# W_out's first blocks prepared early, the MLP entry reordered, the right factors in two pools: a float32 transformer block on one NeuronCore

## The chip, the cores and the metric

The kernel runs as one program on one core of a Trainium2 chip. Its time is the device time of one execution in microseconds, the median over several runs. A profile is taken of one execution. The engines named below are TensorE (PE, matmuls), VectorE (DVE), ScalarE (ACT), GpSimd (POOL) and SyncE (SP, which here only starts DMAs). Each engine works through its own queue in order.

## The reference, cut to what matters

One block of a transformer, 1024 tokens of width 1024, everything in float32. Two attentions (a compressed, selected and windowed one, and a sliding one with sinks) give `o_a` and `o_b`; what follows them is the part that this case is about:

```
y = sigmoid(gate_a) * (o_a @ w_up_nsa) + sigmoid(gate_b) * (o_b @ w_up_swa)
h = h + rms_norm(y @ w_out, norm_mix_post)          # w_out 1024 x 1024
u = rms_norm(h, norm_mlp_pre)
f = square(relu(u @ w_mlp_in)) @ w_mlp_out          # 1024 x 4096, 4096 x 1024
h = h + rms_norm(f, norm_mlp_post)
```

## The kernel before, in words

**Precision.** Every float32 operand is split in two: a part h, which ACT rounds to the matmul's format, and a rest l = value - h, which DVE (sometimes POOL) subtracts. A product then is three matmuls, h·h, h·l and l·h (`split`, L84; `mm3`, L123). So each weight and each activation needs an ACT and a DVE instruction before PE can use it.

**Stages around the change.** (1) The gates' loop (L752): for each of eight 128-wide column blocks `dc`, the up-projections of both attentions, times the gates, split into `yh`, `yl`, one pair for the first 512 tokens (pool y0) and one for the last 512 (pool y1). (2) `out_proj` (L813), called four times with two token blocks of 128 each: it goes through W_out in eight row blocks of 128x1024. `load_w` (L96) brings a block into one of two raw places (`wraw`), ACT rounds it to `wh`, and the rest `wl` is cut between DVE and POOL in the first two calls and made by DVE alone after that. 12 matmuls use a block. (3) The norms of each token block `b`: `norm_a` adds the residual, `norm_b` scales by the second norm (L864), `norm_t` transposes on PE into the right factors of the MLP. (4) The first MLP product, `u @ w_mlp_in`, by seven products per pair of 128-column blocks instead of eight (Strassen-Winograd); 16 pairs `p`, each product 12 matmuls (`prod`, L956). Products 1 and 2 of the first four pairs (`head`, L965) need only the first 512 tokens and are issued early, between the transposes. Products 5, 3, 6, 4, 7 (`mlp1`, L1004) need right factors `bh[i]`, `bl[i]` that DVE builds from the transposes of the last tokens (`factor`, L888), and sums and differences of W_in's columns, which POOL builds (L1014, L1041). The pairs 0 and 1 run in step with the four `factor` calls; the others follow one by one. (5) The second MLP product, from L1093, works through seven products of eight 256-deep steps `kc`. Each step splits a piece of W_out of the MLP (`vh`, `vl`) and a stored piece of the first product (`fh`, `fl`), all in pool st2 with NG = 4 places of each kind.

**What sets the order.** The Tile framework orders each engine's queue with a timeline simulation, along the program's order as far as data allow. `tc.issue_after(i)` keeps instructions of i's engine behind i. Pools are stacks on the left and the right side of SBUF; a new pool overlays a closed one, and a tile waits for the old tiles that lie in its place. u1 (L929) held bh5, bl5, bh3, bl3, bh6, bl6, bh4, bl4 (8 KB each per partition) and then the two places of 8 KB that carry b12, b22 and later bh7, bl7: 80 KB from the right end. st2, 64 KB from the same end, so lies on bh3 to bl4 and on bh7, bl7.

Of the kernel before, what the change touches and what calls it, by code (L numbers as in the profile page):

```python
# [52 lines left out]
def tile_hybrid_block(ctx: ExitStack, tc: tile.TileContext, x, norm_mix_pre, norm_mix_post, norm_mlp_pre,  # L53
# [688 lines left out]
    with ExitStack() as s:  # L742
# [3 lines left out]
        yl = [p.tile([P, NB, 512], F32R, name="yl", tag="yl") for p in yp]  # L746
        s_ps = s.enter_context(ExitStack())
# [58 lines left out]
        we = s_we.enter_context(pool("we"))  # L806
        wor = w_out.rearrange("(k p) c -> p k c", p=P)
# [3 lines left out]
        started = []  # L811

        def out_proj(c, ts_, nhs, xs_=(), at=0):  # L813
            pss = {(t, nh): ps_any() for t in ts_ for nh in nhs}
            n = 1024 // (512 * len(nhs))
            for k2 in range(NB // n):
                wh, wl = load_w([(None, wor[:, n * k2:n * k2 + n, 512 * nhs[0]:512 * nhs[-1] + 512])],
                                [n, 512 * len(nhs)], *((wp2, 2) if not started else (we, WEB)), cut=CUT[c], rpool=wp2, l_eng="dve" if c else None)
# [4 lines left out]
                for j in range(n):  # L823
                    k = n * k2 + j
                    for t in ts_:
                        ts = slice(t * P, (t + 1) * P)
                        for i, nh in enumerate(nhs):
                            ns = slice(i * 512, (i + 1) * 512)
                            mm3(pss[t, nh], yh[c][:, k, ts], yl[c][:, k, ts], wh[:, j, ns], wl[:, j, ns],
                                k == 0, k == NB - 1)  # L830
            started.append(1)
            for t in ts_:
# [4 lines left out]
                for nh in nhs:  # L837
                    ns = slice(nh * 512, (nh + 1) * 512)
                    junk = we.tile([P, 512], F32, name="junk", tag="junk", bufs=1)
# [3 lines left out]
        ss2s = {}  # L843

# [16 lines left out]
        def norm_b(b):  # L861

            r2 = rstd_of(ep, ss2s[b])
            nc.vector.scalar_tensor_tensor(o1[b], hbs[b], r2, gpre, op0=ALU.mult, op1=ALU.mult)  # L864

        def norm_t(b):
# [16 lines left out]
            nc.vector.tensor_tensor(t1, pts[0], braw[b % 4, 0], op=ALU.subtract)  # L883
# [44 lines left out]
        s_u2r = s.enter_context(ExitStack())  # L928
        u1 = s_u2r.enter_context(pool("u1", side="right"))  # L929
        bh, bl = {}, {}  # L930
        for i in (5, 3, 6, 4):
            bh[i] = u1.tile([P, 4, 512], F32R, name=f"bh{i}")
            bl[i] = u1.tile([P, 4, 512], F32R, name=f"bl{i}")
# [13 lines left out]
        norm_a(7)  # L947
        norm_t(4)
# [16 lines left out]
        def head(p, fp_, whl):  # L965
# [10 lines left out]
            nc.vector.scalar_tensor_tensor(c11, c11, 0.0, c11, op0=ALU.max, op1=ALU.mult)  # L976
            nc.sync.dma_start(f_d[0][p], c11)
# [13 lines left out]
        for b in range(4):  # L991
            factor(3, b)
# [10 lines left out]

        def mlp1(p):  # L1004
            raw = []
            for e in range(2):
                r = wp2.tile([P, NB, P], F32, name="wraw", tag="wraw", bufs=2) if e == 0 else \
                    w1a.tile([P, NB, P], F32, name="wraw2", tag="wraw2", bufs=2)
                c0 = (2 * p + e) * P
                nc.sync.dma_start(r, w_mlp_in[:, c0:c0 + P].rearrange("(k p) c -> p k c", p=P))  # L1010
                raw.append(r)
            a11, a12, a21, a22 = raw[0][:, 0:4], raw[0][:, 4:8], raw[1][:, 0:4], raw[1][:, 4:8]
            sm = w1a.tile([P, 4, P], F32, name="ws", tag="ws", bufs=3)
            nc.gpsimd.tensor_tensor(sm, a21, a22, op=ALU.add)  # L1014
            early = p in pre
            if early:
                xb, c11, _ = pre[p]
                s1 = f5.tile([P, 512], F32, name="p5", tag="p5", bufs=2)
                nc.scalar.activation(s1, xb, AF.Copy)
# [20 lines left out]
            for o, i0, i1 in ((sm, sm, a11), (a12, a12, sm), (a21, a11, a21)):  # L1040
                nc.gpsimd.tensor_tensor(o, i0, i1, op=ALU.subtract)  # L1041
# [53 lines left out]
        st2 = s.enter_context(pool("st2", side="right"))  # L1095
        pq = s.enter_context(pool("ps3", space=PSUM))
# [50 lines left out]
        def product(i, bank, first, last):  # L1147

            n = NG if last and i == 7 else 1
            for k0 in [*range(NK - n), NK - n]:  # L1150
                ks = range(k0, k0 + (n if k0 == NK - n else 1))
                hl = {}
                for kc in ks:
                    src = operand(i, kc)
                    vh = st2.tile([P, 2, 512], F32R, name="vh", tag="vh", bufs=NG)
                    vl = st2.tile([P, 2, 512], F32R, name="vl", tag="vl", bufs=NG)
# [117 lines left out]
```

## Time and profile before

| | |
|---|---|
| median of 3 runs | 1553.06 us (1552.43 to 1554.15) |
| profiled execution | 1550.25 us, span 1548.5 us |
| PE busy | 1475.5 us, 95% of the span |
| DVE, ACT, POOL busy | 68%, 51%, 23% |
| mean granted clock of PE | 0.985 |

PE busy means that a matmul was under way; at the lower clock a matmul takes longer and still counts as busy. Idle time of PE, or busy time at the lower clock, is what a change can win. Of the 40 slices (38.7 us each) into which the page cuts the span, PE has 9 tenths or more in most; in the stages that the change touches it has 8 tenths in four (from 735, 813, 968 and 1200 us) and 6 in one (from 890 us).

### The profile page before, as it was taken

How to read it: one execution, taken by the hardware profiler on the slowest of the kernel's cores; microseconds unless marked ns; L12 is line 12 of the kernel's file. 1: busy time of each engine (PE TensorE's matmuls, PEld its weight loads, DVE VectorE, ACT ScalarE, POOL GpSimd, SP SyncE). 2: the span in 40 equal slices, each digit the busy share in tenths (PEclk: the TensorE clock that was granted, in tenths of full speed). 3: DMA queues.
4: the chain of work that ended last, by engine and by line, in shares of the span. 5: the costliest groups of instructions: out<-in, count | busy, mean ns of one | idle time of the engine just before them, and what ended most of it. 6: DMA issues, size and time to landing. Idle time of an engine off the chain costs nothing.

```text
span 1548.5 us, 19945 instructions
## 1 busy us (share of the span) xinstructions
PE 1475.5 (95%) x6920; PEld 1208.1 (78%) x6920; DVE 1053.7 (68%) x2086; ACT 788.3 (51%) x1525; POOL 362.6 (23%) x290
## 2 busy tenths in 40 slices
PE   6998999999999999999898969899999899999997
PEld 5897888788887788888766757688888688888886
DVE  5555774598855988646547798787667555594775
ACT  5344675598854988654346663233322334334533
POOL 3000342100001000041052035676556300000302
PEclk9999999999999999999999979999999999999999
DMA  7733125111132111174356633444444697353551
GB/s 218 252 98 87 35 50 158 46 35 41 36 99 61 40 35 42 32 257 148 108 192 233 221 116 107 155 148 166 157 137 144 220 359 270 99 194 102 164 176 55
DMA packets 162037, 204.79 MB, mean 132 GB/s; under 512 B 15120, under 2 KB 105264, under 8 KB 161936
## 3 DMA queue, kind: packets, MB, share of 16 engines
q1 hardware_dynamic: 154224, 180.68, 36.8%
q0 software_dynamic: 6992, 20.48, 3.8%
q10 hardware_dynamic: 720, 2.36, 0.4%
q8 instruction: 54, 0.88, 0.2%
q14 instruction: 47, 0.39, 0.1%
HBM read 153.02 MB, written 58.32 MB: 136 GB/s over the span
## 4 chain that ended last, share of the span: by engine, by line
PE 69%; issue 8%; DVE 6%; POOL 3%; DMA 2%; ACT 2%; DVEq 0%; POOLq 0%; ACTq 0%
PE xs L1167 10%; PE ys L1167 8%; PE mm L124 5%; PE mm L126 5%; PE mm L125 5%; PE ps L959 5%; PE ps L961 5%; PE ps L960 5%; PE pt L522 5%; PE o L535 2%; PE o L534 2%; PE s L489 2%; DMA wraw<-in_w_out_dram 2%; PE s L490 2%; PE ps L124 2%
## 5 line engine op out<-in xcount | busy, mean ns | idle before, releaser
L124 PE MATMUL mm<-uh,wh 128*128 128x512 f32 x464 | 200.2, 431 | 5.3 <-DVE qb L448 3.2
L125 PE MATMUL mm<-ul,wh 128*128 128x512 f32 x464 | 183.9, 396 | 0.0
L126 PE MATMUL mm<-uh,wl 128*128 128x512 f32 x464 | 183.7, 396 | 0.0
L91 DVE TENSOR_TENSOR tl<-pt,th 128x512 fp32r<-128x512 f32 x162 | 110.6, 687 | 42.1 <-ACT th L87 41.2
L91 POOL TENSOR_TENSOR wl<-wraw,wh 128x1024 fp32r<-128x1024 f32 x16 | 38.4, 2403 | 417.1 <-ACT wh L87 385.2
L502 ACT ACTIVATE e<-e,nm 128x256 f32<-128x256 f32 (+7 forms) x192 | 124.3, 649 | 20.0 <-DVE nm L496 19.5
L87 ACT ACTIVATE fh<-fraw 128x1024 fp32r<-128x1024 f32 x56 | 59.4, 1063 | 146.1 <-PE xs L1167 78.5
L87 ACT ACTIVATE wh<-wraw 128x1024 fp32r<-128x1024 f32 x69 | 73.1, 1059 | 113.9 <-PE mm L125 36.7
L87 ACT ACTIVATE th<-pt 128x512 fp32r<-128x512 f32 (+1 forms) x178 | 104.4, 593 | 50.6 <-PE pt L522 43.1
L91 DVE TENSOR_TENSOR fl<-fraw,fh 128x1024 fp32r<-128x1024 f32 x56 | 69.3, 1243 | 78.3 <-ACT fh L87 78.3
L1167 PE MATMUL xs<-vl,fh 128*128 128x512 f32 x256 | 100.7, 393 | 4.2 <-DVE vl L91 4.2
L126 PEld LDWEIGHTS mm<-uh,wl 128*128 128x128 f32 x464 | 87.4, 188 | 20.7
L124 PEld LDWEIGHTS mm<-uh,wh 128*128 128x128 f32 x464 | 88.0, 190 | 18.4 <-issue 3.3
L522 PE MATMUL pt<-ident,e 128*128 128x128 f32 x648 | 101.1, 273 | 0.3 <-DVE tl L91 0.2
L91 DVE TENSOR_TENSOR wl<-wraw,wh 128x1024 fp32r<-128x1024 f32 x53 | 69.7, 1315 | 46.0 <-ACT wh L87 45.8
L1167 PE MATMUL xs<-vh,fl 128*128 128x512 f32 x256 | 100.4, 392 | 0.0
L1167 PE MATMUL xs<-vh,fh 128*128 128x512 f32 x256 | 100.1, 392 | 0.0
L125 PEld LDWEIGHTS mm<-ul,wh 128*128 128x128 f32 x464 | 88.3, 190 | 11.9
L522 PEld LDWEIGHTS pt<-ident,e 128*128 128x128 f32 x648 | 80.7, 140 | 18.4 <-issue 0.9
L1190 POOL TENSOR_TENSOR cc<-cc,gB 128x512 f32<-128x512 f32 x14 | 24.3, 1762 | 268.9 <-ACT sq L1189 267.2
L87 ACT ACTIVATE ws_h<-wraw 128x512 fp32r<-128x512 f32 x48 | 30.1, 629 | 107.1 <-PE ps L960 104.8
L959 PE MATMUL ps<-bh,ws_h 128*128 128x512 f32 x192 | 76.3, 397 | 3.9 <-ACT ws_h L87 1.7
(287 smaller groups left out, 4046.4 us busy)
## 6 DMA issues: line engine op xcount, KB each, us to landing
fraw<-f_d SPq DMA_DIRECT2D x48, 512.0 KB, 3.5
wraw<-in_w_mlp_in_dram SPq DMA_DIRECT2D x36, 512.0 KB, 4.4
wraw<-in_w_out_dram SPq DMA_DIRECT2D x32, 512.0 KB, 3.6
f_d<-q SPq DMA_DIRECT2D x64, 256.0 KB, 3.7
b<-in_w_mlp_out_dram SPq DMA_DIRECT2D x32, 512.0 KB, 10.8
wraw<-in_w_in_dram SPq DMA_DIRECT2D x27, 512.0 KB, 4.6
f_d<-c SPq DMA_DIRECT2D x48, 256.0 KB, 4.3
gate_d<-gst SPq DMA_DIRECT2D x32, 256.0 KB, 2.0
```

What stands on the lines that cost most here:

```text
L87: nc.scalar.activation(h, src, AF.Copy)
L91: eng.tensor_tensor(l, src, h.bitcast(F32), op=ALU.subtract)
L124: nc.tensor.matmul(ps, ah, bh, start=first, stop=False)
L125: nc.tensor.matmul(ps, ah, bl, start=False, stop=False)
L126: nc.tensor.matmul(ps, al, bh, start=False, stop=last)
L489: nc.tensor.matmul(ps[:, :w], qs[r][:, qcol], kh, start=True, stop=False)
L502: nc.scalar.activation(e[:, :n], e[:, :n], AF.Exp, scale=-1.0, bias=nm[:, r:r + 1], accum_out=sm[:, r:r + 1])
L522: tr = nc.tensor.transpose(pt[:rows, r, :], es[r][:, off:off + rows], ident)
L959: nc.tensor.matmul(ps, ah[:, k, :], bh[i][:, k, :], start=n[0], stop=False, skip_group_check=True)
L960: nc.tensor.matmul(ps, ah[:, k, :], bl[i][:, k, :], start=False, stop=False, skip_group_check=True)
L961: nc.tensor.matmul(ps, al[:, k, :], bh[i][:, k, :], start=False, stop=n[1], skip_group_check=True)
L1167: nc.tensor.matmul(bank[t], l_[:, j, ts], r_[:, j, :], start=a_, stop=z_, skip_group_check=True)
```

## The change

Five edits. (a) The first two W_out blocks are loaded during the gates' loop (at dc = 5), and the first is split there, into a pool `wo` of its own; the first `out_proj` call splits the second block itself and loads the other six. (b) The right factors lie in two pools, u1a with bh5, bh3, bh6 and u1 with bh4 and b12/b22/bh7, and the second product's splits in two, st2 with three places of each kind and st3 with one. (c) `norm_b(6)` and `norm_b(7)` stand ahead of `norm_t(4)`; the factors' instructions are kept behind the last `norm_b` or the last transposed difference, and behind the copy L1019. (d) Relu and square of the first four heads go from one DVE to two ACT instructions, their stores from SP's to POOL's queue, and the sums and differences of pairs 0 and 1 from POOL to DVE. (e) The W_in columns of pairs 0 to 3 are loaded ahead of the pairs, those of 2 and 3 into the places of `wh`, `wl` that the heads leave.

```diff
+        wo = s_wo.enter_context(pool("wo", side="right"))
+        def wo_load(k):
+            r = wo.tile([P, 1, 1024], F32, name="wraw", tag="wraw", bufs=2)
+            nc.sync.dma_start(r, wor[:, k:k + 1, :])
+            wo_raw.append(r)
...
+                if dc == 5:
+                    wo_load(0)
+                    wo_load(1)
+                    wo_hl += [wo.tile([P, 1, 1024], F32R, name=n, tag=n) for n in ("wh", "wl")]
+                    split(*wo_hl, wo_raw[0])
...
             for k2 in range(NB // n):
-                wh, wl = load_w(...)
+                if started or k2 > 1:
+                    wh, wl = load_w(...)
+                elif k2:
+                    wh, wl = (wp2.tile([P, 1, 1024], F32R, name=n_, tag="w" + n_[1], bufs=2) for n_ in ("wh", "wl"))
+                    split(wh, wl, wo_raw[1])
+                else:
+                    wh, wl = wo_hl
...
+        u1a = s_u2r.enter_context(pool("u1a", side="right"))
         u1 = s_u2r.enter_context(pool("u1", side="right"))
         for i in (5, 3, 6, 4):
-            bh[i] = u1.tile([P, 4, 512], F32R, name=f"bh{i}")
+            bh[i] = (u1 if i == 4 else u1a).tile([P, 4, 512], F32R, name=f"bh{i}")
...
         norm_a(6)
         norm_a(7)
+        norm_b(6)
+        norm_b(7)
         norm_t(4)
...
-            nc.vector.scalar_tensor_tensor(c11, c11, 0.0, c11, op0=ALU.max, op1=ALU.mult)
-            nc.sync.dma_start(f_d[0][p], c11)
+            if p < NPRE:
+                nc.scalar.activation(c11, c11, AF.Relu)
+                nc.scalar.activation(c11, c11, AF.Square)
+            else:
+                nc.vector.scalar_tensor_tensor(c11, c11, 0.0, c11, op0=ALU.max, op1=ALU.mult)
+            (nc.gpsimd if p < NPRE else nc.sync).dma_start(f_d[0][p], c11)
...
             if p == 0:
                 norm_t(5)
-                norm_b(6)
-                norm_b(7)
...
-        for b in range(4):
-            factor(3, b)
+        with tc.issue_after(last_norm[0].ins):
+            for b in range(4):
+                factor(3, b)
...
+        def load_raw(p):
+            raw = {}
+            for e in (1, 0):
+                pool_, tag = ((w1a, "wraw2") if e else (wp2, "wraw")) if p > 3 else \
+                    ((wp2, "wraw"), (w1a, "wraw2"), (wp2, "w" + "hl"[e]), (wp2, "w" + "hl"[e]))[p]
+                raw[e] = pool_.tile([P, NB, P], F32, name="wraw", tag=tag, bufs=2)
+                c0 = (2 * p + e) * P
+                nc.sync.dma_start(raw[e], w_mlp_in[:, c0:c0 + P].rearrange("(k p) c -> p k c", p=P))
+            return raw
+        raws = {p: load_raw(p) for p in range(NPRE)}
...
-            nc.gpsimd.tensor_tensor(sm, a21, a22, op=ALU.add)
+            diff = nc.vector if p < 2 else nc.gpsimd
+            with tc.issue_after(last_t[0].ins):
+                diff.tensor_tensor(sm, a21, a22, op=ALU.add)
...
-                nc.gpsimd.tensor_tensor(o, i0, i1, op=ALU.subtract)
+                diff.tensor_tensor(o, i0, i1, op=ALU.subtract)
...
-            for b in range(4 if i else 0):
-                factor(i, b)
+            with tc.issue_after(last_t[0].ins), tc.issue_after(last_s1[0].ins):
+                for b in range(4 if i else 0):
+                    factor(i, b)
...
+        st3 = s.enter_context(pool("st3", side="right"))
+        def st_tile(name, kc):
+            p, n = (st3, 1) if kc % NG == NG - 1 else (st2, NG - 1)
+            return p.tile([P, 2, 512], F32R, name=name, tag=name, bufs=n)
...
-            h = st2.tile([P, 2, 512], F32R, name="fh", tag="fh", bufs=NG)
-            l = st2.tile([P, 2, 512], F32R, name="fl", tag="fl", bufs=NG)
+            h, l = st_tile("fh", kc), st_tile("fl", kc)
```

`last_norm`, `last_t` and `last_s1` hold the latest DVE instruction of `norm_b` (L864), of `norm_t` (L883) and the latest ACT copy L1019. The pool `we` is opened after the first `out_proj` call, when `wo` is closed.

## Rows read from the trace of the kernel before

**Rows 1.** The page's first part: busy time, share, instructions of each engine.

```profile
PE 1475.5 (95%) x6920; PEld 1208.1 (78%) x6920; DVE 1053.7 (68%) x2086; ACT 788.3 (51%) x1525; POOL 362.6 (23%) x290
```

**Rows 2.** Stretches: length, busy PE, PEld, DVE, ACT, POOL (instructions), granted clock, DMA share, GB/s.

```profile
768.90:800.20 31.30, 25.70 (x97) 19.92 (x96) 8.84 (x11) 9.83 (x10) 13.11 (x8) 0.89 0.59 204
800.20:883.80 83.60, 76.29 (x329) 57.04 (x328) 61.84 (x111) 51.61 (x91) 16.79 (x14) 1.00 0.66 226
883.80:907.80 24.00, 23.89 (x112) 19.63 (x112) 23.59 (x47) 18.08 (x36) 1.06 (x2) 1.00 0.56 167
907.80:933.80 26.00, 12.41 (x40) 8.92 (x37) 25.39 (x30) 14.61 (x27) 12.69 (x8) 0.67 0.21 61
933.80:960.00 26.20, 26.20 (x112) 20.66 (x113) 18.50 (x23) 8.05 (x14) 12.58 (x9) 1.00 0.35 102
960.00:1010.00 50.00, 44.13 (x178) 33.42 (x177) 36.95 (x36) 13.03 (x22) 34.66 (x22) 0.97 0.48 154
1224.00:1237.05 13.05, 8.08 (x25) 6.14 (x25) 10.48 (x12) 5.56 (x7) 2.17 (x3) 0.74 0.71 247
```

**Rows 3.** Waits of PE from 660 to 1010: total us, times, longest.

```profile
PE ps L124 <- ACT wh L108: 7.2, 6, 4.5
PE pt L874 <- DVE o L864: 5.9, 2, 4.7
PE ps L959 <- ACT p L1019: 4.3, 1, 4.3
PE ps L961 <- DVE s_l L91: 3.7, 1, 3.7
```

**Rows 4.** Timeline, PE, first W_out call: start, us, line, operation, [idle before, releaser].

```profile
773.44 2.07 PE L124 MATMUL ps<-wh,yh 128*128 128x512 f32 x4 [4.49 <-ACT wh L108]
...
784.70 1.10 PE L124 MATMUL ps<-wh,yh 128*128 128x512 f32 x4
...
787.50 1.10 PE L124 MATMUL ps<-wh,yh 128*128 128x512 f32 x4
```

**Rows 5.** Timeline of SP's queue, ACT and POOL in the same call.

```profile
768.31 50.89 SPq L100 DMA_DIRECT2D wraw<-in_w_out_dram  x15
...
772.33 1.06 ACT L108 ACTIVATE wh<-wraw 128x1024 fp32r<-128x1024 f32 x1 [1.26 <-DMA wraw<-in_w_out_dram]
...
786.52 1.66 POOL L116 TENSOR_TENSOR wl<-wraw,wh 128x384 fp32r<-128x384 f32 x1 [1.58 <-ACT wh L108]
```

**Rows 6.** DMA issues of the page: count, KB each, median us to landing.

```profile
wraw<-in_w_out_dram SPq DMA_DIRECT2D x32, 512.0 KB, 3.6
```

**Rows 7.** Timeline, DVE, at the MLP's entry.

```profile
911.34 1.28 DVE L864 SCALAR_TENSOR_TENSOR o<-hb,rs_o,gpre 128x1024 f32<-128x1024 f32 x1
...
914.49 0.68 DVE L896 TENSOR_TENSOR braw<-b_l,braw 128x512 f32<-128x512 f32 x1
...
920.88 1.75 DVE L895 TENSOR_TENSOR b_l<-b_l,b_h 128x512 f32<-128x512 f32 x1
```

**Rows 8.** Groups by line, DVE, 883.8 to 934.8: count, busy us, mean ns, idle before.

```profile
L91 DVE TENSOR_TENSOR bl<-braw,bh 128x512 fp32r<-128x512 f32 x8 | 7.5, 953 | 0.0
...
L976 DVE SCALAR_TENSOR_TENSOR c<-c 128x512 f32<-128x512 f32 x4 | 2.7, 680 | 0.0
```

**Rows 9.** Groups by line, POOL, the same stretch.

```profile
L1041 POOL TENSOR_TENSOR ws<-ws,wraw 128x512 f32<-128x512 f32 x2 | 3.3, 1666 | 2.5 <-DVE s_l L91 2.5
```

**Rows 10.** Line L1014 (POOL): what its idle time waited for, us, times.

```profile
  DMA wraw<-in_w_mlp_in_dram: 55.4, 14
```

**Rows 11.** Waits of SP's queue, 880 to 1010: total us, times, longest.

```profile
SPq L1010 <- DVE ws_l L91: 51.9, 10, 21.7
```

**Rows 12.** Timeline at the second product's start: ACT, DVE, PE.

```profile
1221.14 1.06 ACT L87 ACTIVATE fh<-fraw 128x1024 fp32r<-128x1024 f32 x1 [2.15 <-PE ps L961]
...
1229.85 1.22 DVE L91 TENSOR_TENSOR fl<-fraw,fh 128x1024 fp32r<-128x1024 f32 x1
...
1232.26 0.79 PE L1167 MATMUL xs<-vl,fh 128*128 128x512 f32 x1 [4.23 <-DVE vl L91]
```

More of the change, by code (lines that the diff above doesn't have):

```diff
@@ L746, in tile_hybrid_block @@
         yl = [p.tile([P, NB, 512], F32R, name="yl", tag="yl") for p in yp]
+        s_wo = s.enter_context(ExitStack())
+        wo = s_wo.enter_context(pool("wo", side="right"))
+        wor = w_out.rearrange("(k p) c -> p k c", p=P)
+        wo_raw, wo_hl = [], []
+        def wo_load(k):
+            r = wo.tile([P, 1, 1024], F32, name="wraw", tag="wraw", bufs=2)
+            nc.sync.dma_start(r, wor[:, k:k + 1, :])
+            wo_raw.append(r)
         s_ps = s.enter_context(ExitStack())
@@ L805, in tile_hybrid_block @@
         s_we = s_e.enter_context(ExitStack())
-        we = s_we.enter_context(pool("we"))
-        wor = w_out.rearrange("(k p) c -> p k c", p=P)
         ssp = [ep.tile([P, 2], F32, name="ssp", tag="ssp", bufs=8) for _ in range(NB)]
         hbs = {}
-        started = []
+        started, we = [], []
         def out_proj(c, ts_, nhs, xs_=(), at=0):
@@ L816, in out_proj @@
             for k2 in range(NB // n):
-                wh, wl = load_w([(None, wor[:, n * k2:n * k2 + n, 512 * nhs[0]:512 * nhs[-1] + 512])],
-                                [n, 512 * len(nhs)], *((wp2, 2) if not started else (we, WEB)), cut=CUT[c], rpool=wp2, l_eng="dve" if c else None)
+                if started or k2 > 1:
+                    wh, wl = load_w([(None, wor[:, n * k2:n * k2 + n, 512 * nhs[0]:512 * nhs[-1] + 512])],
+                                    [n, 512 * len(nhs)], *((we[0], WEB) if started else (wp2, 2)), cut=CUT[c],
+                                    rpool=wp2, l_eng="dve" if c else None)
+                elif k2:
[3 more added lines that the diff above has]
+                    wh, wl = wo_hl
                 if k2 == at:
@@ L830, in out_proj @@
                                 k == 0, k == NB - 1)
+            if not started:
+                s_wo.close()
+                we.append(s_we.enter_context(pool("we")))
             started.append(1)
@@ L838, in out_proj @@
                     ns = slice(nh * 512, (nh + 1) * 512)
-                    junk = we.tile([P, 512], F32, name="junk", tag="junk", bufs=1)
+                    junk = we[0].tile([P, 512], F32, name="junk", tag="junk", bufs=1)
                     nc.scalar.activation(junk, pss[t, nh], AF.Square, accum_out=ssp[b][:, nh:nh + 1])
@@ L843, in tile_hybrid_block @@
         ss2s = {}
+        last_norm, last_t, last_s1 = [None], [None], [None]
         def load_x(b, eng=None):
@@ L863, in norm_b @@
             r2 = rstd_of(ep, ss2s[b])
-            nc.vector.scalar_tensor_tensor(o1[b], hbs[b], r2, gpre, op0=ALU.mult, op1=ALU.mult)
+            last_norm[0] = nc.vector.scalar_tensor_tensor(o1[b], hbs[b], r2, gpre, op0=ALU.mult, op1=ALU.mult)
         def norm_t(b):
@@ L882, in norm_t @@
             t1 = eh.tile([P, 4, P], F32, name="t1", tag="hb", bufs=2)
-            nc.vector.tensor_tensor(t1, pts[0], braw[b % 4, 0], op=ALU.subtract)
+            last_t[0] = nc.vector.tensor_tensor(t1, pts[0], braw[b % 4, 0], op=ALU.subtract)
             nc.scalar.activation(b12[:, :, bs], pts[0], AF.Copy)
@@ L931, in tile_hybrid_block @@
         for i in (5, 3, 6, 4):
-            bh[i] = u1.tile([P, 4, 512], F32R, name=f"bh{i}")
-            bl[i] = u1.tile([P, 4, 512], F32R, name=f"bl{i}")
+            bh[i] = (u1 if i == 4 else u1a).tile([P, 4, 512], F32R, name=f"bh{i}")
+            bl[i] = (u1 if i == 4 else u1a).tile([P, 4, 512], F32R, name=f"bl{i}")
         def u7(name, dt):
@@ L1002, in ab @@
                     p_.tile([P, 4, P], F32R, name=tag + "l", tag=tag + "l", bufs=bufs))
-        def mlp1(p):
[L1005 to L1011, printed above, removed]
+        def load_raw(p):
[8 more added lines that the diff above has]
+        raws = {p: load_raw(p) for p in range(NPRE)}
+        def mlp1(p):
+            raw = raws[p] if p in raws else load_raw(p)
             a11, a12, a21, a22 = raw[0][:, 0:4], raw[0][:, 4:8], raw[1][:, 0:4], raw[1][:, 4:8]
             sm = w1a.tile([P, 4, P], F32, name="ws", tag="ws", bufs=3)
-            nc.gpsimd.tensor_tensor(sm, a21, a22, op=ALU.add)
+            diff = nc.vector if p < 2 else nc.gpsimd
+            with tc.issue_after(last_t[0].ins):
+                diff.tensor_tensor(sm, a21, a22, op=ALU.add)
             early = p in pre
@@ L1018, in mlp1 @@
                 s1 = f5.tile([P, 512], F32, name="p5", tag="p5", bufs=2)
-                nc.scalar.activation(s1, xb, AF.Copy)
+                last_s1[0] = nc.scalar.activation(s1, xb, AF.Copy)
             else:
@@ L1154, in product @@
                     src = operand(i, kc)
-                    vh = st2.tile([P, 2, 512], F32R, name="vh", tag="vh", bufs=NG)
-                    vl = st2.tile([P, 2, 512], F32R, name="vl", tag="vl", bufs=NG)
+                    vh, vl = st_tile("vh", kc), st_tile("vl", kc)
                     hl[kc] = f_op(i, kc) + (vh, vl)
```

## Prediction

> **What bounds the kernel now.** The page's first part comes first: PE is busy for 1475.5 of 1548.5 us [rows 1], so whatever this change wins it wins from the 73 us in which PE is idle, and from matmuls that ran at the lower clock. Next come the stretches [rows 2], to find where those losses lie. The price of a matmul there comes from the timeline: two W_out blocks of 12 matmuls each begin at 784.70 and 787.50 [rows 4], so a matmul of 512 columns costs 2.80 / 12 = 0.233 us when nothing is late. What each stretch takes beyond its matmuls at that price is its loss:
>
> - 768.9 to 800.2, the first W_out call: 96 matmuls are 22.4 us of 31.3; lost 8.9.
> - 800.2 to 883.8, the other three calls: 329, of them 40 transposes, which I price at half a matmul (an estimate); 72.1 of 83.6; lost 11.5.
> - 907.8 to 960.0, from the last head to the end of the first pairs: 152, of them 16 transposes; 33.6 of 52.2; lost 18.6.
> - 960 to 1010: 178 are 41.5 of 50; lost 8.5.
> - 1224 to 1237, the turn to the second product: 25 are 5.8 of 13.05; lost 7.2.
>
> Third, the waits of PE [rows 3] say what ended last in them: ACT's rounding of the first W_out block (4.5 us at once), `norm_b`'s output (4.7 us), the copy L1019 (4.3 us) and DVE's rest `s_l` (3.7 us). Each gap is followed by matmuls at the lower of the two clocks, 1.2 GHz: the granted clock is 0.89, 0.67 and 0.74 in the stretches with gaps and 1.00 in those without [rows 2]. A gap removed gives back this part too, and the loss figures hold it. Four of the five losses are aimed at by the change: 8.9 + 18.6 + 8.5 + 7.2 = 43.2 us.
>
> **(a) First W_out blocks.** Now SP can start the first W_out load only at 768.31, since its place lies on the attention outputs that the gates' last matmuls read; ACT begins at 772.33 [rows 5] and PE at 773.44 after 4.49 us of idleness [rows 4]. With block 0 split at dc = 5, PE goes on at 769. Block 1 needs only its split: 1.06 us of ACT [rows 5] and 1.22 us of DVE [rows 12], within the 2.8 us of block 0; at worst ACT takes the gates' last `yh` first and PE waits 0.6 us (an estimate). The two loads (3.6 us each [rows 6]) and block 0's split are hidden by the gates' loop, where PE never waits for ACT or DVE; without that cover they would cost about 2.4 us. Can the loads of blocks 2 and on follow? The chain of one raw place is load 3.6, ACT 1.06, POOL 1.66 [rows 5, 6], 6.3 us for every second block or 3.2 per block against PE's 2.8. So this ring falls behind by 0.4 us a block, but it starts two blocks ahead: it has 14 blocks in the first two calls instead of 16, which is 6.3 us, plus the raw places, which come free about 2 us earlier (they now lie on operands that the gates read earlier in their last group). By the ring the gain is 8.3 us, by PE's loss it is at most 8.9. Bounds 5 and 9; I take 7.5.
>
> **(b) Two pools.** At the second product's start PE waits 4.23 us for `vl`, behind `fl` at 1229.85 [rows 12]. The place of `fl` was bh7's, which the last product reads to its end; `fh` lay on bh4 and started at 1221.14 when product 4 let go [rows 12]. With 48 KB for st2 on the 48 KB of u1a, the first three steps' splits wait for products 5, 3 and 6 alone, and only step 3 (16.8 us of matmuls later) waits for product 7. So `fl` and `vl` of step 0 can run in product 7's 2.8 us: 2 x 1.22 us [rows 12], just enough. The price: DVE's queue may still hold the last pair's evictions ahead of them, worth 1 to 3 us. At the entry bh5 and b12/b22 now lie on y1, which the last W_out call reads to its end, instead of on free ground; the instructions that write them came after that end anyway, so I put 0 to 1 us on it. Bounds 1 and 7; I take 6 of 7.2.
>
> **(c, d) The entry.** From 883.8 to 933.8 DVE is busy for 23.59 + 25.39 = 49.0 of 50 us [rows 2], and does its work in the wrong order: `norm_b(7)` came at 911.34 [rows 7], after many factors that PE needed only from 934 on, while the last transposes, on which every factor product hangs, waited for it. With both `norm_b` ahead and the factors held behind, norm, eviction and `norm_t` work up to the last transposed difference fits into the 24 us of heads. Then DVE's total: less L976, 2.7 us [rows 8] (ACT takes eight instructions for it, 0.6 us each by estimate from 1.06 for twice the width [rows 5], and has 17 idle us in the two stretches [rows 2]); plus eight differences at 0.68, 5.4 us; less what POOL cost it. That last term is read off the same operations: 0.68 us alone, 1.75 beside POOL's [rows 7], and a mean of 0.953 for the eight `bl` [rows 8]. POOL's eight differences (12.69 us in 907.8 to 933.8 [rows 2], 1.67 each [rows 9]) could so stretch eight DVE operations by 1.07, up to 8.6 us. So 49.0 - 2.7 + 5.4 - 8 = 43.7 us if POOL stays quiet. After the heads 43.7 - 24 = 20 us are left, plus 12 further splits and evictions, 8 us, against the 10 x 2.8 = 28 us of the products of pairs 0 and 1: balanced, with a hand-over of 2 to 4 us at the first product and some lateness at product 6, whose factor needs three DVE operations per token block. I leave 8.6 of the 18.6 lost: gain 10, bounds -5 (the order makes DVE wait) and 16.
>
> The stores of the four heads go past SP's queue, where they stood between W_in loads, to POOL's, which has 1.06 us of work in the 24 us of heads [rows 2]; nothing of POOL's is late for them.
>
> The Trainium skill ("SBUF — State Buffer", section "Who interferes with whom") says that a DVE instruction with two SBUF inputs and a GpSimd instruction that reads SBUF lock each other out, whichever starts first. Here DVE's 1.75 us beside POOL's 1.67 agree [rows 7, 9]. The rule speaks against (e) as much as for (d): the differences of pairs 2 and 3 stay on POOL and now find their data early. By it the first rival below holds; by the rows of the quiet DVE alone the sum above does.
>
> **(e) W_in columns.** POOL sat 55.4 us in 14 waits for these loads [rows 10], and SP held them back for 51.9 us until DVE had finished with a place [rows 11]. With the places of `wh` and `wl`, free when heads 2 and 3 are done, pairs 2 and 3 load by the end of the heads, at 908, and no longer wait for pairs 0 and 1; pairs 4 and 5 find the places of those two. A load then is early by more than one pair (19.6 us). What is late next is DVE beside POOL, busy 36.95 and 34.66 of 50 us [rows 2]. On SP's queue the eight loads stand in a row and a late place holds those behind it, which are later pairs. Of 8.5 lost I take 4.5 as gained; bounds 0 and 8.
>
> **Sum.** 7.5 + 6 + 10 + 4.5 = 28.0. The profiled execution took 1550.25, so 1522.25; the runs' median lies 2.8 above it, so 1525.
>
> **Rivals.**
> 1. Contention comes back at the entry. Pairs 2 and 3 have four differences that wait for no split; beside DVE's factors they add 4 x 1.07 = 4.3 us, all eight 8.6, where DVE has no slack. For: DVE at 49.0 of 50 [rows 2]. Against: POOL could work while DVE reads PSUM. Then entry 3 and W_in columns 2.5: 7.5 + 6 + 3 + 2.5 = 19, 1534.
> 2. DVE keeps ahead throughout and nearly every aimed loss goes: 8.5 + 7 + 15 + 7.5 = 38, 1515. For: DVE falls to 18.50 of 26.2 just after [rows 2]. Against: the narrow handing over between ACT and DVE for each split.
> 3. It doesn't do what it says: the planner still puts the last transposes behind the heads, and `fl` behind the last evictions. Entry 2, pools 1.5: 7.5 + 2 + 1.5 + 4.5 = 15.5, 1537.5. For: it is what the queues held before [rows 7, 12]. Against: the edits fix that order by hand.
> 4. Slower: the factors, held behind the last transposed difference, run in series. If that difference comes at 914 as now (L896 on its factor at 914.49 [rows 7]), 52 DVE operations at 0.68 and 8.6 of contention end at 958, and with hand-overs (6) and the last products (5.6) pairs 0 and 1 end at 970, against about 956 now (136 matmuls are 11.3 products by 960). That is 14 us, and 5 more if the gaps hold the clock at 1.2 GHz; (e) is then worth nothing. 19 - 7.5 - 6 = 5.5 slower, 1558.5. It decides from the point where the last transposes wait for the fourth head and DVE has nothing else to do. Against: DVE then would idle ahead of 914, and the norms ahead exclude just that.
>
> **How the numbers follow.** Forecast (1519 to 1530) 0.58, rival 1 0.20, rival 2 0.08, rival 3 0.09, rival 4 0.05. The range takes in the forecast, rival 2, rival 1 and part of rival 3: 1514 to 1540. A measurement of this kernel tells 0.2% (3.1 us) from no change. Forecast and rivals 1 to 3 lie below that; of rival 4 I put one part in five on a draw. With 0.01 of rival 3 also put there, faster is 0.94, same 0.02, slower 0.04.
>
> **What would show it.** In the profile after: PE has no gap ahead of its first W_out matmul and no lower clock there; the two L864 of blocks 6 and 7 stand on DVE before the second head ends; PE's waits for L864, L1019 and `s_l` are below 5 us together; POOL's L1014 waits less than 30 us for loads; the wait at the second product's start is below 1.5 us. The prediction is wrong if the losses of 907.8 to 960 merely move to the next stretch, if DVE shows new 1.75 us operations among the factors, or if the three later W_out calls lose more than 11.5 us and give (a) back.

## The result and the profile after

The changed kernel takes 1536.62 us (median of 4 runs, 1535.4 to 1538.22) against 1553.61 before; ratio 0.9892, interval 0.9875 to 0.9909. Timed once more on another chip it took 1538.79 against 1552.87, ratio 0.991 (0.9894 to 0.9926). So it is faster by 14 to 17 us; forecast were 28 (1525), and 1534 was what the first rival gave. The profile after is of an execution of 1536.7 us with a span of 1534.9.

First come the page's busy times, then the stretches, cut at about the same places of the program as in [rows 2] (columns as there):

```profile
PE 1472.4 (96%) x6920; PEld 1205.2 (79%) x6920; DVE 1044.1 (68%) x2090; ACT 793.1 (52%) x1533; POOL 347.5 (23%) x284
```

```profile
768.90:795.00 26.10, 24.52 (x104) 18.66 (x102) 8.51 (x11) 9.58 (x11) 10.31 (x7) 1.00 0.62 220
795.00:878.70 83.70, 76.34 (x328) 56.56 (x327) 61.65 (x112) 50.81 (x90) 16.34 (x14) 1.00 0.65 224
878.70:903.50 24.80, 24.80 (x121) 20.30 (x119) 21.48 (x43) 19.62 (x42) 2.70 (x5) 1.00 0.75 221
903.50:960.00 56.50, 40.11 (x147) 30.20 (x146) 51.02 (x64) 26.55 (x46) 24.42 (x16) 0.85 0.32 95
960.00:1010.00 50.00, 50.00 (x217) 40.33 (x216) 41.42 (x45) 17.26 (x27) 35.19 (x24) 1.00 0.43 148
```

The first W_out call and 960 to 1010 are mended: the clock is 1.00 and PE is busy nearly throughout. What is left of the entry's loss stands in 903.5 to 960: PE is busy for 40 of 56.5 us, DVE for 51. PE's waits from 660 to 1010, which answer to [rows 3] (L1060 was L1019, L899 was L874, L990 was L961), say the same:

```profile
PE ps L988 <- ACT p L1060: 9.3, 1, 9.3
PE ps L988 <- ACT ws_h L87: 3.5, 2, 2.4
PE ps L124 <- ACT wh L108: 3.0, 5, 1.2
PE ps L990 <- DVE ws_l L91: 2.4, 2, 2.1
...
PE pt L899 <- DVE rs_t L147: 1.2, 1, 1.2
```

The wait for the norm (4.7 at once before) is gone and the copy's has grown from 4.3 to 9.3. DVE's timeline at the end of the heads shows why (start, length, line, operation, idle time before it):

```profile
902.75 0.69 DVE L908 TENSOR_TENSOR t<-pt,braw 128x512 f32<-128x512 f32 x1 [1.94 <-PE pt L899]
903.36 0.68 DVE L1055 TENSOR_TENSOR ws<-wraw 128x512 f32<-128x512 f32 x1
907.98 0.69 DVE L1055 TENSOR_TENSOR ws<-wraw 128x512 f32<-128x512 f32 x1 [3.94 <-DMA wraw<-in_w_mlp_in_dram]
908.59 1.89 DVE L920 TENSOR_TENSOR b_l<-b_l,b_h 128x512 f32<-128x512 f32 x3
910.40 0.68 DVE L1004 TENSOR_TENSOR c<-ps,s 128x512 f32<-128x512 f32 x1
911.00 0.68 DVE L1082 TENSOR_TENSOR wraw<-wraw 128x512 f32<-128x512 f32 x1
911.60 0.68 DVE L91 TENSOR_TENSOR bl<-t,bh 128x512 fp32r<-128x512 f32 x1
```

Pair 1's sum stands at the head of DVE's queue and waits 3.94 us for its columns. Three factor differences follow (one row, L920), and only behind them come the sum of head 3 (L1004) and block 7's `bl`. ScalarE's queue waits for the sum of head 3: its ReLU and square stand there ahead of the copy that PE needs. PE starts at 912.97. At the second product the wait for `vl` (4.23 [rows 12]) has become one for the PSUM bank that the last pair's copy frees:

```profile
PE xs L1214 <- ACT c L1099: 2.3, 1, 2.3
```

To see where time is won, I take the start of the k-th matmul in each profile; all have 6920. The numbers are "before minus this one", in us (positive: earlier than before). The 4200th (counted from 0) stands just ahead of the heads and the 4700th where PE no longer waits. The second product starts at the 5576th; the 5780th and the 5850th lie on both sides of a wait in it that is shown under banks_swapped. The labels are those of the runs in the next section.

```
k:                  500  3750  3800  4100  4200  4700  5780  5850 | 4200 to 4700
changed            -0.1  -1.1  +6.4  +4.9  +5.0 +10.4 +14.5 +13.8 |  5.4
changed_again      -0.9  -2.1  +5.4  +2.1  +2.1  +7.9 +10.4 +10.4 |  5.8
loads_in_order     -1.9  -2.0  +5.5  +4.0  +3.1 +10.3 +14.5 +14.5 |  7.2
order_and_no_copy  -1.4  -1.4  +6.2  +3.4  +3.0 +10.6 +14.7 +14.4 |  7.6
banks_swapped      -1.2  -2.1  +5.4  +2.8  +2.1  +8.4 +15.1 +13.1 |  6.3
only_a_b           -1.8  -2.7  +4.9  +3.0  +2.9  +4.2 +10.9  +4.6 |  1.3
entry_undone       -2.5  -3.3  +4.2  +0.8  -2.0  +3.8  +6.3  +6.3 |  5.8
no_early_columns   -0.9  -1.4  +6.1  +4.2  +3.5  +8.5 +15.2 +12.8 |  5.0
pairs_on_dve       -0.4  -0.4  +7.1  +6.5  +2.0  +9.3 +13.5 +13.0 |  7.3
chain_first        -1.1  -1.2  +6.3  +3.9  +3.0 +13.2 +15.8 +15.8 | 10.2
factor_held        -2.0  -2.5  +5.0  +2.7  +2.4  +6.7  +9.5  +9.5 |  4.3
chain_and_pairs    -2.8  -3.7  +3.9  +2.1  +1.5 +15.5 +18.1 +18.1 | 14.0
pair2_behind       -0.5  -1.7  +5.9  +2.5  +1.9 +16.4 +23.1 +18.4 | 14.5
```

Up to the gates' loop nothing was changed; at the 3750th, in its last part, every profile lies 0.4 to 3.7 us behind that of before, whose execution (1550.25) was one of the shorter ones of its kernel (median 1553.61). So single stretches are compared, not sums. About 0.5 us of the last column is chance, by the one repeat that there is (changed against changed_again). The column starts at the 4200th since PE waits between the 4100th and there for a W_out block in code that is the same: 0.85, 0.83 and 1.88 us in changed, changed_again and banks_swapped. That wait was 2.48 us in entry_undone and 2.78 in pairs_on_dve, and while PE stands the other engines can get ahead; so for these two the column may flatter. From the 4100th they gain 3.0 and 2.8 us, the changed kernel 5.5 and 5.8.

### The profile page after: what moved, and what is told of

Read it like the earlier page. It is cut to its first block, busy times and chain, and to the rows that moved or that the text cites. A ratio compares the mean times of both kernels' runs of the same rounds, so it can differ in the third digit from the quotient of the medians.

```text
span 1534.9 us, 19943 instructions
## 1 busy us (share of the span) xinstructions
PE 1472.4 (96%) x6920; PEld 1205.2 (79%) x6920; DVE 1044.1 (68%) x2090; ACT 793.1 (52%) x1533; POOL 347.5 (23%) x284
## 4 chain that ended last, share of the span: by engine, by line
PE 79%; DVE 8%; DMA 7%; ACT 3%; issue 2%; POOL 1%; SPq 0%; DVEq 0%; ACTq 0%; POOLq 0%
PE ys L1214 8%; PE xs L1214 8%; PE mm L124 7%; PE mm L125 7%; PE mm L126 7%; PE ps L990 6%; PE ps L988 6%; PE ps L989 6%; PE pt L522 5%; DMA wraw<-in_w_out_dram 3%; PE o L535 2%; PE ps L125 2%; PE ps L126 2%; PE ps L124 2%; PE o L534 2%; PE s L489 2%
## 5 line engine op out<-in xcount | busy, mean ns | idle before, releaser
L91 DVE TENSOR_TENSOR wl<-wraw,wh 128x1024 fp32r<-128x1024 f32 x55 | 68.2, 1240 | 48.4 <-ACT wh L87 48.1
```

The costliest lines, as they stand in the source:

```text
L91: eng.tensor_tensor(l, src, h.bitcast(F32), op=ALU.subtract)
```

## Experiments

Three theories were tried on the entry's missing gain. Theory 1: VectorE's queue order behind the last transposes, with pair 1's late columns, takes it. Theory 2: VectorE's work, stretched beside GpSimd's, takes it. Theory 3: ScalarE's queue, which got ReLU and square, takes it. Timed ratios are against the kernel before, on the same chip. Line numbers in the variants differ by up to 8.

**loads_in_order**

```diff
-raws = {p: load_raw(p) for p in range(NPRE)}
+raws = {p: load_raw(p) for p in range(2)}
+with tc.issue_after(last_ld[0].ins):          # last load of pair 1
+    raws.update({p: load_raw(p) for p in range(2, NPRE)})
```

> Only SyncE's queue changes: the two loads of W_in columns of pair 1 stand ahead of the two of pair 2; every other engine issues what the changed kernel issues, in the same order. Theory 1 (the entry loses because DVE's queue stands 3.94 us for pair 1's columns and all behind it comes late): the stand falls below 1 us, and the chain behind it (three factor differences 1.89, the sum of head 3 0.68, ReLU and square on ScalarE 1.3, copy 0.6) ends near 909 instead of 912.97, so TensorE's wait after the heads falls from 9.3 to 5 to 6 us and the kernel ends 3.5 to 4.5 us before the changed one: about 1532.5. Theory 2 (VectorE's order and its port conflict with GpSimd decide, and an earlier start only moves the loss): the wait falls the same way, but the gaps of 924 to 944 grow, and the 4600th matmul starts within 1 us of where it does in the changed kernel: 1536. If the places of pair 1 come free no earlier than its loads are issued now (897.6 and 900.1), the gain is at most the 2 to 3 us that the loads of pair 2 take from theirs.

Measured: 1537.24, ratio 0.9896 (0.9878 to 0.9914). DVE's wait for pair 1's columns is gone, but PE's wait falls only to 7.46 us. DVE's timeline at the same place:

```profile
905.26 1.28 DVE L1058 TENSOR_TENSOR ws<-wraw 128x512 f32<-128x512 f32 x2
906.46 2.96 DVE L920 TENSOR_TENSOR b_l<-b_l,b_h 128x512 f32<-128x512 f32 x3
909.35 0.68 DVE L1004 TENSOR_TENSOR c<-ps,s 128x512 f32<-128x512 f32 x1
909.95 0.68 DVE L1085 TENSOR_TENSOR wraw<-wraw 128x512 f32<-128x512 f32 x1
910.54 1.75 DVE L91 TENSOR_TENSOR bl<-t,bh 128x512 fp32r<-128x512 f32 x1
```

L920 takes 2.96 where it took 1.89, `bl` 1.75 where it took 0.68: GpSimd's two operations on pair 2 now run beside them (907.42 and 909.95). Of the 3.94 us, 2.1 are paid back so. Theory 1 named a real wait and was too simple; theory 2's mechanism is in the rows.

**order_and_no_copy**

```diff
-s1 = f5.tile(...); last_s1[0] = nc.scalar.activation(s1, xb, AF.Copy)
+s1 = pre[p][2]      # pair 0: the head's own copy; one c11 buffer fewer
```

> As loads_in_order, and pair 0 keeps the first copy of its product from the heads, so that ScalarE's second copy of it (which stands behind ReLU and square of head 3 in ScalarE's queue) goes. Theory 3 (ScalarE's queue, with head 3's ReLU and square moved to it, sets the entry): TensorE's first matmul after the heads starts when s_h is there, 905.6, a wait of 2 to 3 us, and the kernel ends 2.5 to 3.5 us before loads_in_order. Theory 1 (VectorE's queue sets it): block 7's low part of the factor, the last of eight instructions in VectorE's queue, ends only 0.7 us before the copy does in the changed kernel, so the second matmul waits for it and the gain over loads_in_order is 0.5 to 1.5 us: 1531.5.

Measured: 1536.97, ratio 0.9891 (0.9875 to 0.9908). PE starts earlier and then stands for `bl`, as theory 1 had it. From 4200 to 4700 it gains 7.6 us against 7.2 in loads_in_order. Theory 3 falls.

```profile
908.32 0.50 PE L988 MATMUL ps<-bh,s_h 128*128 128x512 f32 x1 [2.04 <-ACT s_h L87]
912.79 0.80 PE L989 MATMUL ps<-bl,s_h 128*128 128x512 f32 x1 [3.97 <-DVE bl L91]
```

**banks_swapped**

```diff
+ys = [pq.tile([P, 512], F32, name=f"ys{t}") for t in range(4)]
 xs = [pq.tile([P, 512], F32, name=f"xs{t}") for t in range(4)]
-ys = [pq.tile([P, 512], F32, name=f"ys{t}") for t in range(4)]
```

> The accumulators of the second product trade places in PSUM: the four that are written first get the banks that were free longer; the order on all engines stays. If the 2.3 us that TensorE waits at the start of the second product for the last pair's evacuation (a bank still in use) is all that is late there, the wait goes and the kernel ends 1.5 to 2.3 us earlier, 1534.5. Rival: the operands are no earlier than the bank (the last splits end within 1 us of it), and the gain is under 0.5 us.

Measured: 1539.23, ratio 0.9906 (0.9888 to 0.9924). The bank's wait is gone and nothing takes its place there: PE goes into the second product without a gap.

```profile
1219.19 0.39 PE L1214 MATMUL xs<-vh,fh 128*128 128x512 f32 x1
```

So the operands were in time, and the rival is wrong about them. From the 4700th to the 5780th this profile gains 6.7 us, the changed kernel's two 4.1 and 2.5. But 51 us into the product, at the 5792nd, PE waits for an operand whose rounding on ACT waits for a load, and 2.0 us go again:

```profile
PE ys L1214 <- ACT fh L87: 1.7, 1, 1.7
```

```profile
1268.91 1.06 ACT L87 ACTIVATE fh<-fraw 128x1024 fp32r<-128x1024 f32 x1 [4.43 <-DMA fraw<-f_d]
```

```profile
1235.00:1275.00 40.00, 38.31 (x170) 31.36 (x169) 25.52 (x22) 16.50 (x18) 0.00 (x0) 1.00 1.05 384
```

The DMA engines are busy throughout this stretch (384 GB/s; the view counts their share as 1.05). The three other profiles without the bank's wait have the same wait for `fh` there, 3.2 us (only_a_b), 2.1 (no_early_columns) and 2.9 (pair2_behind), and all three gain 6.7 us up to it; among the others it is 0.4 us at most. So what is won at the start of the second product is in good part lost again to its loads. The run's time is no shorter than the changed kernel's; whether anything of the 1.5 to 2.3 us that were expected stays is not shown.

**entry_undone, no_early_columns, only_a_b**: parts of the change, taken back in the code (c and d in the first; e in the second; c, d and e in the third).

> The changed kernel with the entry's edits taken back: last norms behind the second head, no holds on the factors, ReLU and square of the heads' c11 on VectorE, their stores and the differences of all pairs on the old engines; the early W_out blocks, the two pools and the early W_in columns stay. If the entry's edits lose the 4.2 us that the changed kernel lies behind between the 4200th and the 4500th matmul, and the early columns gain their 8.3 us without them, it ends at 1532. If the early columns gain only because GpSimd was relieved of the first two pairs, the gain of the stretch up to the 4700th matmul shrinks to 4 us or less and it ends at 1537 to 1541.

> Edits a, b, c and d without e: the W_in columns of pairs 0 to 3 are loaded where the kernel before loads them. entry_undone (a, b, e) gained 3.0 us between the 4100th and the 4700th matmul against the kernel before, the changed kernel (all) 5.5. If the two are independent, this one gains 2.5 there and ends near 1541. If the entry's edits bring nothing without the early columns, because pair 1's sum then waits longer on VectorE, it gains 0 or loses, and ends at 1543 to 1545. If the early columns are what makes VectorE stand and spoil the entry, it gains 5 or more: 1538.

> Only the early W_out blocks and the two pools of right factors; entry and columns as in the kernel before. Early blocks: 7.5 us at the first W_out call, 1.2 to 3.4 given back in the later calls; nothing between the 4100th and the 4700th matmul (within 1 us); 2.5 to 4 us at the second product. End 1543 to 1545. A gain of over 2 us in the entry would mean that the pools do more there than hold places.

Measured: 1538.27 (0.99, 0.9882 to 0.9918), 1538.41 (0.9902, 0.9888 to 0.9915) and 1543.88 (0.9939, 0.9927 to 0.9952). From 4200 to 4700: a, b alone 1.3 us; with e 5.8; with c, d 5.0; with all 5.4 and 5.8. **By this column either part is worth about 4 us, and both together no more than one.** The profiles alone don't prove it: that of entry_undone is of its longest execution (1543.92), and from the 4100th on its e is worth 1.8 us. The runs' times carry it: only_a_b is some 5.5 us longer than each of the other two, which are equal to each other and within the intervals of the changed kernel. The changed kernel's two times are 7.3 and 5.1 us under only_a_b; two parts that add would have given 11. What the entry's edits take away can be seen in PE's waits of entry_undone, 890 to 1010:

```profile
PE pt L899 <- DVE o L889: 6.6, 1, 6.6
PE ps L986 <- ACT p L1058: 4.6, 1, 4.6
PE ps L986 <- ACT ws_h L87: 3.7, 1, 3.7
```

In no_early_columns the copy's wait is 5.3 us, not 9.3: it is the early columns that bring it to 9.3.

**pairs_on_dve**

```diff
-diff = nc.vector if p < 2 else nc.gpsimd
+diff = nc.vector if p < 4 else nc.gpsimd
```

> The sums and differences of pairs 2 and 3 go from GpSimd to VectorE too, so that GpSimd computes nothing until pair 4. VectorE gets eight instructions of 0.60, 4.8 us, and loses the stretching (instructions of 1.75 in place of 0.68 at 926 to 942 and their like: 7.9 us together). Theory 2 (the conflict with GpSimd is what the entry's gain went into): VectorE's work falls by about 3 us, waits of TensorE between 920 and 945 shrink, the 4700th matmul starts 2 to 3 us earlier, 1534. Rival: VectorE's own order decides, the eight instructions stand ahead of what is due, and it ends at 1536 to 1538.

Measured: 1534.03, ratio 0.987 (0.9854 to 0.9885); DVE's busy time in 903.5 to 960 falls from 51.0 to 49.0 us with eight instructions more. Its sums and differences of 128x512 that took over 0.9 us there lasted 9.9 us beyond 0.68 each in the changed kernel, 2.6 here. The wait after the heads stays 9.6. The run's time is the one that theory 2 gave, though its interval overlaps with that of the changed kernel's first timing (0.9875 to 0.9909). Its profile is of the longest of four executions (1537.49) and decides nothing: from 4200 to 4700 it gains 1.7 us more than the mean of the changed kernel's two, from the 4100th on 2.8 us less. So theory 2 holds in size by the run, and by the stretching in the rows.

**chain_first**

```diff
-with tc.issue_after(last_t[0].ins):                        # sums
+with tc.issue_after((last_bl if p else last_t)[0].ins):    # pair 1 on: behind block 7's bl
-with tc.issue_after(last_t[0].ins), tc.issue_after(last_s1[0].ins):    # factors
+with tc.issue_after(last_sl[0].ins), tc.issue_after(last_s1[0].ins):   # behind pair 1's s_l
```

> As loads_in_order, and in VectorE's queue the four instructions that TensorE waits for (sum of pair 0, sum of head 3, low part of block 7's factor, low part of pair 0's left factor) stand ahead of pair 1's sum and of the differences of the factor of product 6, which are held behind them. From the last transposes on the chain is five instructions of 0.6 on VectorE, then ReLU, square and copy on ScalarE: TensorE's wait after the heads is 3 to 4.5 us instead of 9.35 in the changed kernel and 7.46 in loads_in_order. Theory 1/3 (queue order at the entry costs the time): what is won stays, the 4700th matmul starts 4 to 5 us before that of the changed kernel's, 1532. Theory 2 (VectorE's work between the heads and 950, 51.0 of 56.5 us in the changed kernel, some 8 us of it instructions stretched beside GpSimd, is the bound): the held differences come late in their turn, the waits of 920 to 945 grow by as much, and the 4700th matmul is within 1.5 us of the changed kernel's, 1536.

Measured: 1536.06, ratio 0.9887 (0.9873 to 0.99). PE's waits, 890 to 1010, and three of DVE's instructions:

```profile
PE ps L990 <- DVE ws_l L91: 8.1, 3, 6.2
PE ps L988 <- ACT p L1063: 3.6, 1, 3.6
```

```profile
908.27 1.76 DVE L91 TENSOR_TENSOR s_l<-ws,s_h 128x512 fp32r<-128x512 f32 x1
...
910.55 1.76 DVE L91 TENSOR_TENSOR bl<-b_l,bh 128x512 fp32r<-128x512 f32 x1
...
922.34 1.75 DVE L91 TENSOR_TENSOR ws_l<-wraw,ws_h 128x512 fp32r<-128x512 f32 x1
```

The wait falls from 9.35 to 3.6 as computed; 6.2 us come back as a wait for `ws_l`, which itself is stretched beside GpSimd. From 4200 to 4700 it gains 10.2 us. Both theories hold a part; the run's time alone doesn't tell it from the changed kernel's.

**factor_held**

```diff
-for i in (6, 4, 7, 0, 0):            # factor i after each step of the pairs
+for fs in ((), (6, 4), (7,), (), ()):   # and last_sl is product 3's
```

> chain_first, and the differences and sums of product 6's factor are held further, behind the low parts of product 3's left factors of both pairs. Theory 2 (VectorE's total work before product 6 is the bound, about 27 instructions of 0.6 beside 10.9 us of matmuls): the wait of 6.2 us for the low part falls under 3, and a wait of 5 to 9 us for the factor opens ahead of product 6; the 4700th matmul starts within 2 us of chain_first's. Theory 1 (order alone): the waits of the stretch fall by 3 us or more together, and it ends 3 us before chain_first.

Measured: 1541.03, ratio 0.9924 (0.9908 to 0.9941): a miss of both.

```profile
PE ps L988 <- ACT bh L87: 8.7, 1, 8.7
PE ps L989 <- DVE bl L91: 5.6, 1, 5.6
```

The 6.2 us become 14.3. The wait for `ws_l` goes, as theory 2 had it (0.2 us are left), but the waits for the factor are 14.3 us where it had 5 to 9. The factor's first differences start 7.2 us later (L920 at 920.59, 913.44 in chain_first), and one of its roundings then stands in ScalarE's queue behind this instruction, which waits for a sum on GpSimd:

```profile
930.85 0.63 ACT L87 ACTIVATE s_h<-ws 128x512 fp32r<-128x512 f32 x1 [5.31 <-POOL ws L1058]
```

That sum started at 923.76 and took 7.06 us, while VectorE's instructions followed one another without a gap until 929.70; a sum of that kind took 1.26 us while VectorE stood (904.93 in the changed kernel). From 931.5 to 942 VectorE's part of the factor ran stretched beside GpSimd. A hold can cost more than the order that it mends.

**chain_and_pairs**: the diffs of chain_first and pairs_on_dve.

> chain_first and pairs_on_dve together. In chain_first the entry's wait fell to 3.6 us and the one that took its place is 6.2 us for a left factor's low part, behind VectorE instructions of which four last 1.75 instead of 0.68 beside GpSimd. Theory 2 (VectorE's work, stretched by GpSimd, is what is left): without GpSimd's part VectorE runs two instructions more ahead of that low part (1.2 us) and loses 3 to 4 us of stretching, so the wait falls to about 4 and the 4700th matmul starts 1 to 3 us earlier, counted from the last head, than in chain_first; 1533. Rival (the stretching hit instructions that nobody waited for): the same as chain_first or up to 2 us later, 1536 to 1538.

Measured: **1530.87** (1529.93 to 1532.45), ratio 0.9857 (0.984 to 0.9874); the changed kernel, run beside it (changed_again), has 0.991 (0.9894 to 0.9926), so this one beats both. Waits 890 to 1010, the stretch, and the `ws_l` that PE waits for:

```profile
PE ps L990 <- DVE ws_l L91: 4.7, 3, 4.0
PE ps L988 <- ACT p L1063: 3.5, 1, 3.5
```

```profile
903.50:960.00 56.50, 48.05 (x189) 36.80 (x187) 54.07 (x77) 29.60 (x54) 19.13 (x11) 0.91 0.44 126
```

```profile
921.77 0.68 DVE L91 TENSOR_TENSOR ws_l<-wraw,ws_h 128x512 fp32r<-128x512 f32 x1
```

In the same 56.5 us there are 189 matmuls instead of 147, and the instruction that took 1.75 takes 0.68. From 4200 to 4700 it gains 14.0 us. With the two remedies together c, d and e give 12.7 us over only_a_b, more than with chain_first's (8.9) or pairs_on_dve's (6.0) alone.

**changed_again**

> The changed kernel once more, to see how far two profiles of the same code differ in each stretch. If the differences before the entry (the 500th to the 4300th matmul: up to 3 us between the runs so far) are chance, this one differs there by 1 to 3 us from its first profile too, while the wait after the heads stays 8 to 9.5 us and the time from the last head to the 4700th matmul repeats within 1.5 us. If they are not chance, all repeats within 0.3 us.

Measured: 1538.79. The first 3750 matmuls differ by 1.0 us from the first profile of the same code, the 4100th by 2.8, the wait after the heads is 7.9, and the gain from 4200 to 4700 repeats within 0.4 us. So differences of this size ahead of the entry come without any change of code; nearly all of the first 3750's is there by the 760th matmul, 180 us in.

**pair2_behind**

```diff
-with tc.issue_after((last_bl if p else last_t)[0].ins):
+with tc.issue_after((first_sl if p > 1 else last_bl if p else last_t)[0].ins):  # product 3's ws_l
+ys = [...]; xs = [...]      # as banks_swapped
```

> chain_and_pairs with two more edits in different stretches: pair 2's sum and differences are held behind the low part that TensorE waited 4.0 us for, and the accumulators of the second product trade banks as in banks_swapped. Of pair 2's instructions four (2.4 us at 0.60) stood ahead of that low part: if VectorE's order there is what is left, the wait of 4.0 falls to 1.5 to 2 us, and the time from the last head to the 4700th matmul falls by 2 us. Rival: they are only late in their turn and the waits of 925 to 945 grow by 2 us. The banks: 1 to 1.5 us at the second product, as banks_swapped's profile showed between the 5500th and the 5800th matmul (4.7 us gained there against the kernel before, 2.5 to 4.1 in the others). End 1527 to 1529, with the rival 1530 to 1531.

Measured: 1531.13, ratio 0.9848 (0.9823 to 0.9874): no different from chain_and_pairs. The wait for `ws_l` is 4.01 us again, though it ends 10.75 us after PE's first matmul behind the heads (11.96 in chain_and_pairs): PE came to it earlier. 0.5 us are won from 4200 to 4700 where 2 were expected. At the second product the bank's wait is gone and 6.7 us are gained up to the 5780th, but the wait for the load behind it (2.9 us, with some matmuls at the lower clock after it: the granted clock is 0.96 from 1235 to 1275) leaves 2.0.

## Why the prediction was right and wrong

The sign and the range were right. The size was not: 28 us forecast, 14 to 17 measured. Term by term:

- **(a), 7.5 forecast.** Between the 3750th and the 3800th matmul all thirteen profiles gain 7.5 to 7.6 us. There is no gap ahead of the first W_out matmul and no lower clock behind it, as named. Not foreseen: 0.6 to 3.4 us are given back between the 3800th and the 4100th. In most profiles it goes in the first call (3.5 us by the 3882nd in changed_again, but 0.4 in the changed kernel's own), where PE waits for ACT's rounding of the blocks that follow, 1.6 us in the changed kernel's profile and twice that in changed_again's (768 to 800):

```profile
PE ps L124 <- ACT wh L108: 3.4, 3, 2.1
```

  The ring of raw places, which the prediction credited with 8.3 us, is not always ahead; why one execution loses more there than the next stays open.
- **(b), 6 forecast: at its place 6.7 us (4700 to 5780) in the four profiles without the wait for the bank, 2.5 to 4.2 in the others; at the 5850th 0.4 to 4.7 are left, 3.4 and 2.5 in the changed kernel's two.** `vl` no longer is late, so the mechanism held. Two losses were not in the sum. The bank: the promised wait below 1.5 us is 2.3. The text had half named it ("DVE's queue may still hold the last pair's evictions ahead of them"), but the other way round: a split stands ahead of the last pair's eviction, whose copy frees the bank, which is about 0.8 of the 2.3 us (the eviction starts 1.32 us after the start of its product's last matmul; before the change it was 0.51). The loads: the wait at the 5792nd (banks_swapped above). Nor does every gap bring the lower clock, as the text has it: behind the same 2.3 us the clock is 1.00 from 1205 to 1240 in the changed kernel's first profile and 0.95 in changed_again's.
- **(c, d), 10 forecast, the step that failed.** The text reads: "43.7 us if POOL stays quiet. After the heads 43.7 - 24 = 20 us are left [...] balanced, with a hand-over of 2 to 4 us at the first product". The hand-over was 9.35 us. The sum counted DVE's work, not which instruction waits in its queue, and its term of 8 us for a quiet POOL did not come: in 903.5 to 960 DVE's stretching beside POOL was 9.9 us (12.0 in the same stretch before). In chain_and_pairs the order is mended and POOL takes no sum or difference before pair 4's: there the stretching is 5.0 us, the hand-over 3.5, and 4200 to 4700 gives 14.0 us, 12.7 of them from c, d and e with the two remedies; forecast were 14.5 for c, d and e.
- **(e), 4.5 forecast.** Alone it gave about that: 4.5 us by the column (5.8 - 1.3), 1.8 from the 4100th on, some 5.5 by the runs. The sum treated (c, d) and (e) as independent; beside each other they gave 4.3 us, not 14.5, since the early columns set GpSimd to work on pairs 2 and 3 just where VectorE has no slack, and pair 2's loads stand ahead of pair 1's. SyncE and GpSimd stay held back: 40.9 us in 13 waits for columns (55.4 before [rows 10], below 30 promised):

```profile
  DMA wraw<-in_w_mlp_in_dram: 40.9, 13
```

So the first rival (contention at the entry, 0.20) had the place right and nearly the price (1534), but only a part of the cause. The remedy against contention alone (pairs_on_dve) gave 1.7 us from 4200 to 4700, the remedy of the order with the load ahead (chain_first) 4.6, both together 8.4. Of a load that stops VectorE's queue (e) had said only that a late place holds later pairs on SyncE's queue. One of the text's own signs of being wrong came, 1.75 us operations among the factors, four of them in this row:

```profile
935.82 6.87 DVE L91 TENSOR_TENSOR bh7l<-braw,bh7h 128x512 fp32r<-128x512 f32 x4
```

The other two did not: the losses did not move into 960 to 1010, and the later W_out calls take what they took (83.7 us, 83.6 before). The Trainium skill ("SBUF — State Buffer", section "Who interferes with whom") states the exclusion of the two engines; the trace agrees, 1.75 us against 0.68 for the same instruction with and without GpSimd beside it. `norm_b(7)` came at 895.08, 2.5 us after the second head's sum, a small miss. Block 7's transposes still stood among the last matmuls of the fourth head in PE's queue (DVE idle 1.94 us for them), which is the beginning of rival 4. Whether they can go ahead was not tried.

## What to carry to other kernels

A sum of an engine's work is a bound, not a schedule: after moving work onto an in-order queue, list what stands between the last input and the first output, and ask of each instruction what it may wait for. Two edits aimed at the same loss don't add; forecast the pair by what is left for the second. An operand that is made available earlier sets another engine to work earlier: put its price where it lands. Time won just ahead of a stretch whose loads keep the DMA engines busy throughout can be lost there again: look for the next wait.

## What the runs showed of the hardware

A GpSimd sum of two 128x512 operands in SBUF took 1.26 us while VectorE stood, and 7.10 us while VectorE worked without a gap on operands in SBUF; it ended 1.2 us after VectorE's queue first stood (chain_first, 936.13). So the price of the two engines' exclusion can fall on either side: where both had work in a row, each instruction took about 1.7.

```profile
930.19 7.10 POOL L1058 TENSOR_TENSOR ws<-wraw 128x512 f32<-128x512 f32 x1 [6.65 <-DVE ws_l L91]
```

In the changed kernel SyncE took 2.3 to 2.6 us for the issue instruction of each of the last four of the eight column loads (0.37 for the first three), and the last five of these 512 KB loads landed 7.5 to 10.4 us after their issue, against 4.0 to 5.2 for the first two and for later pairs' loads: early loads in a row come in later each. Profiles of unchanged code differed by up to 3.7 us over the first 760 us, so a single profile's whole span could not have told these variants apart; the stretches could, where PE's waits ahead of them were the same.
